# Adding the residual x to the partial output projection with accumulating DMAs instead of to the finished tiles on VectorE

## The chip, the cores and the metric

The kernel runs on one core of a Trainium2 chip. The metric is the device time of one execution in microseconds (us); a kernel's time is the median of its runs. An engine is named as in the profile: PE is TensorE (PEld its weight loads), DVE is VectorE, ACT is ScalarE, POOL is GpSimd, SP is SyncE. SPq is the queue of DMAs that SP issues.

## The reference

Two sequences, `x_sample` (1024 tokens) and `x_prompt` (512 tokens), each of width 2048, go through one layer and a final norm with the same weights:

```python
def mixer_layer(x, norm_g, w_in, w_dw, b_dw, ln_g, ln_b, w_pw, sink, w_out):
    h = rms_norm(x, norm_g)
    z = h @ w_in                       # split: conv value, glu, gate; q, k, v, attention gate
...
    conv_out = conformer_conv(c_val, c_glu, ...) * silu(c_gate)
    attn_out = banded_sink_attention(q, k, v, sink) * silu(a_gate)
    mix = concatenate([conv_out, attn_out], axis=-1) @ w_out
    return x + mix

def encoder(x, ...):
...
    return rms_norm(x, final_norm_g)
```

All is float32. The change touches one term only: the `x +` in the last line of `mixer_layer`, for `x_sample`.

## The kernel before, in words

Everything is held transposed: a tile has 128 channels on its partitions and tokens along its free dimension. Every float32 operand of a matmul is split into a high and a low part (`Encoder.parts`, lines 434 to 442: ACT copies x into the high part, L438, and DVE subtracts, L439), and a product is three matmuls, high by high, high by low, low by high.

The first sequence (`sample`, `x_sample`) has its large products in `Unit`s (class at line 91). A unit takes two blocks of 128 output channels, two halves of 512 tokens and eight blocks of the 2048 input channels, and computes this two by two by two product with seven products instead of eight (a Strassen-like scheme: sums of weights are made on DVE, L138, and sums of the tokens' operands are made ahead and kept in DRAM). Each of the seven products is twelve matmuls on one PSUM bank (`product`, matmul at L191; banks a, b and c, of which a product of the same unit uses one again). Behind the first matmuls of the next product, `tap` copies the bank to SBUF on ACT (L217) or adds it to a tile there on DVE (`add`, L237). A product that goes on in the same bank has to wait for that copy. Four tiles of 128 by 512 come out of a unit.

Since a unit covers only eight of the sixteen blocks of input channels, there are two units per pair of output blocks. The first one's four tiles are partial sums and are stored to DRAM (`finish`, line 240: `e.store(part, d)`, L432). The second one is `total`: `finish` issues an accumulating DMA on POOL's queue that adds the stored partial tile to the tile in SBUF (`add_into`, L429), and puts the rest of the work into the list `later` with a count. `turn_over` (line 468) is called once per product, lowers the counts, and takes the next step of an entry whose count is up.

The output projection of the first sequence (class `Mix`, line 1119) is eight pairs of output blocks, and so two runs of eight units: `over[0]` with `last` false, on the attention half of the input channels, then `over[1]` with `last` true, on the convolution half. While the first run is on PE, attention of the second sequence runs between its matmuls, and `conv_sums` (line 1165; `block_sums` L1138 to L1141) makes the sums of the convolution half. In the second run the count is `LANDING + 1` = 5 products. When it is up, `project` (L1213) does what is left: it has issued the load of the x tile on SP (L1217) when the accumulating DMA was issued; now DVE adds x (L1220), SP stores the finished tile to `y_d`, and in the next steps ACT squares it (L1227, or L1231 for the first tile) and DVE adds the squares to a running sum (L1229) for the final norm. `Mix.finish` later scales the stored tiles.

Buffers: the tiles that come out of PSUM are taken in turn from two rings of four buffers, `g` and `u` (`Encoder.E`, line 405). `u` also holds attention's queries (loaded at L1005) and outputs (copied at L1066), `g` a difference of weights (L138) in the first run, and both the sums of `block_sums`. The ring `p` of four holds the x tiles, attention's probabilities and operands on their way in. A buffer is used again when all that reads it is done, the store's DMA too.

The order of the instructions on each engine is fixed when the program is built, from the order and the priorities in which they are written: `urgently` and `high_priority` move taps and weight preparation forward, and lanes (`Lane`) hand out side work by an estimated cost per matmul. On SP's queue the DMAs are issued in that fixed order; one that waits for its data holds those behind it.

Of the kernel before, what the change touches and what calls it, by code (L numbers as in the profile page):

```python
# [10 lines left out]
ALU = mybir.AluOpType  # L11
# [22 lines left out]
W = 512  # L34
# [10 lines left out]
NF, NA, NG, NU, NP = 7, 4, 4, 4, 4  # L45
# [45 lines left out]
class Unit:  # L91
# [148 lines left out]
    def finish(self, n):  # L240
        e = self.e
        part, d = self.part[n[0]][n[1]], self.d.pop(n)
        if self.total:

            e.add_into(d, part)
            e.later.append([self.landing, self.done(n[0], n[1], d)])
        else:
            e.store(part, d)


class Plain(Unit):
# [402 lines left out]
class Sequence:  # L654
# [416 lines left out]
    def units(self):  # L1071

        e, w = self.e, self.e.a["w_in"]
        e.low = {}

        def both(cols, name, done):
            part = [[e.tc.dram_tile([P, W], F32, name=f"part_{name}_{t}{c}") for c in range(2)] for t in range(2)]
            keep = [e.tc.dram_tile([P, ND, P], F32, name=f"low_{name}_{c}") for c in range(2)]
            for c in range(2):
                e.low[cols[c]] = (keep[c], c)  # L1080
            return lambda g, last, kind=Unit: kind(e, w, cols, 2 * HALF * g, part, done if last else None, keep if g else None)

        def each(first, second):
            return lambda t, c, z: (first, second)[c](t, z)

        conv = [both((GLU + i, VAL + i), f"conv{i}", self.gated(i)) for i in range(NC)]
        gates = []
        for i in range(0, NC, 2):
            done = each(self.silu_of(self.gate_d[i]), self.silu_of(self.gate_d[i + 1]))
            gates.append(both((GATE + i, GATE + i + 1), f"gate{i}", done))  # L1090
        rest = gates[:2] + [
            both((K + g, V + g), f"kv{g}", each(self.rotate(self.k_d[g]), self.value_of(g))) for g in range(2)
        ]
        for h in range(HEADS):
            turn = self.rotate(self.q_d[h // GROUP][:, h % GROUP])
            rest.append(both((Q + h, AG + h), f"q{h}", each(turn, self.silu_of(self.ag_d[h]))))
        return conv, rest + gates[2:]
# [21 lines left out]
class Mix:  # L1119
# [77 lines left out]
    def units(self):  # L1197
        e = self.e
        out = []
        for o in range(0, ND, 2):  # L1200
            part = [[e.tc.dram_tile([P, W], F32, name=f"part_out{o}_{t}{c}") for c in range(2)] for t in range(2)]
            done = lambda t, c, z, o=o: self.project(o + c, t, z)

            def one(g, last, o=o, part=part, done=done):
                u = Unit(e, e.a["w_out"], (o, o + 1), 2 * HALF * g, part, done if last else None)
                u.late = True
                u.landing = LANDING + 1
                return u

            out.append(one)  # L1210
        return out

    def project(self, o, t, z):  # L1213
        e, nc = self.e, self.e.nc
        cols = slice(t * W, t * W + W)
        x = e.PT("p", NP, [W])
        nc.sync.dma_start(x, self.seq.xT[o][:, cols])  # L1217

        def steps():
            nc.vector.tensor_tensor(z, z, x, ALU.add)  # L1220
            e.store(self.y_d[o][:, cols], z)
            yield
            if not self.summed:
                self.sv = e.F([2, W])
            s = self.sv[:, t]
            if t in self.summed:
                nc.scalar.activation(x, z, AF.Square)  # L1227
                yield
                nc.vector.tensor_tensor(s, s, x, ALU.add)  # L1229
            else:  # L1230
                nc.scalar.activation(s, z, AF.Square)  # L1231
            self.summed.add(t)
            yield

        return steps()
# [615 lines left out]
```

## Time and profile before

| what | value |
|---|---|
| median of 3 runs | 2130.25 us |
| lowest and highest | 2127.07 and 2131.83 us |
| the profiled execution's own time | 2123.9 us |
| its span, first to last instruction | 2122.1 us |
| mean granted TensorE clock | 0.998 |
| DMA | 465.17 MB, 219 GB/s over the span |
| SP's queue (hardware), POOL's queue (software) | 60.6% and 9.0% of 16 engines |

A line of a group of instructions reads: source line, engine, operation, tile written <- tiles read, shapes, count, then busy us and mean ns of one, then the idle time of the engine just before them and what released it. In a timeline the first two numbers are the start and the duration in us, and the brackets at the end hold the idle time before and its releaser. In the list of waits the numbers are the us in total, how often, and the longest. In a table by stages each engine has its busy us and its number of instructions; then come the granted clock, the mean busy share of the 16 DMA engines and GB/s. A row of DMA issues has the count, the size and the median us from issue to landing.

### The profile page before, as it was taken

To read this page: it belongs to the slowest core of one execution; us is meant where nothing else is said; L and a number is where in the kernel's file an instruction comes from. 1 tells how busy PE (TensorE), PEld (TensorE's weight loads), DVE (VectorE), ACT (ScalarE), POOL (GpSimd) and SP (SyncE) were. 2 spreads that over 40 slices of the span, in tenths; PEclk is the share of its full clock that TensorE was granted. 3 is DMA by queue.
4 is the path that set the end of the run, shared out by engine and by line. 5 is a ranking of instruction groups with operands and counts; after the bars stand their busy time and mean duration, and the time that the engine had idled before them with its cause. 6 is when DMAs were issued, how large, how long until landed. Compare 5 with 4: busy or idle time off the path is not lost. (4 is left out here: it accounts for less than half of the span.)

```text
span 2122.1 us, 26838 instructions
## 1 busy us (share of the span) xinstructions
PE 2080.0 (98%) x9330; PEld 1709.6 (81%) x9330; DVE 1710.3 (81%) x2611; ACT 1064.6 (50%) x1736; POOL 105.1 (5%) x124
## 2 busy tenths in 40 slices
PE   8999999999999999899999999999999989999998
PEld 7878888888888888688888888878888867888886
DVE  8758799988899999899987776677899667987543
ACT  7475445333554444544556766345544564563232
POOL 0001110000011111000000000000000001110000
PEclk9999999999999999999999999999999999999999
DMA  8888878754677767754464547987765369799952
GB/s 286 310 286 243 231 179 277 265 190 155 227 215 178 185 161 194 240 183 144 151 219 157 192 157 235 323 291 255 249 238 199 105 208 269 192 306 314 309 172 80
DMA packets 236408, 465.17 MB, mean 219 GB/s; under 512 B 22128, under 2 KB 79856, under 8 KB 236272
## 3 DMA queue, kind: packets, MB, share of 16 engines
q1 hardware_dynamic: 218992, 431.99, 60.6%
q0 software_dynamic: 17280, 31.46, 9.0%
q8 instruction: 73, 1.20, 0.2%
q14 instruction: 63, 0.52, 0.1%
HBM read 319.19 MB, written 144.18 MB: 218 GB/s over the span
## 5 line engine op out<-in xcount | busy, mean ns | idle before, releaser
L191 PE MATMUL a<-t,hl 128*128 128x512 f32 x2640 | 634.3, 391 | 15.5 <-ACT u L217 6.0
L191 PEld LDWEIGHTS a<-t,hl 128*128 128x128 f32 x2640 | 494.7, 188 | 123.4 <-ACT u L217 9.2
L438 ACT ACTIVATE hl<-raw 128x1024 fp32r<-128x1024 f32 (+1 forms) x330 | 296.2, 898 | 367.8 <-DVE raw L138 66.7
L439 DVE TENSOR_TENSOR hl<-raw,hl 128x1024 fp32r<-128x1024 f32 (+1 forms) x330 | 337.6, 1023 | 171.0 <-ACT hl L438 167.0
L906 DVE SCALAR_TENSOR_TENSOR f<-f,c_w_dw,f 128x1024 f32<-128x1024 f32 (+1 forms) x464 | 456.0, 1011 | 1.8 <-ACT f L901 1.6
L578 PE MATMUL a<-t,hl 128*128 128x512 f32 x1344 | 329.0, 394 | 2.6 <-DVE f L848 2.2
L191 PE MATMUL c<-t,hl 128*128 128x512 f32 x1320 | 320.1, 390 | 1.6 <-ACT g L217 0.9
L578 PEld LDWEIGHTS a<-t,hl 128*128 128x128 f32 x1344 | 248.8, 188 | 53.8 <-DVE f L848 2.6
L191 PEld LDWEIGHTS c<-t,hl 128*128 128x128 f32 x1320 | 247.4, 188 | 54.0 <-ACT g L217 1.8
L578 PE MATMUL c<-t,hl 128*128 128x512 f32 x672 | 167.4, 395 | 0.0
L578 PE MATMUL b<-t,hl 128*128 128x512 f32 x672 | 162.2, 392 | 0.8 <-DVE hl L439 0.8
L191 PE MATMUL b<-t,hl 128*128 128x512 f32 x660 | 161.1, 390 | 0.0
L578 PEld LDWEIGHTS b<-t,hl 128*128 128x128 f32 x672 | 125.1, 188 | 26.1 <-DVE hl L439 1.2
L578 PEld LDWEIGHTS c<-t,hl 128*128 128x128 f32 x672 | 124.2, 188 | 24.5
L191 PEld LDWEIGHTS b<-t,hl 128*128 128x128 f32 x660 | 123.4, 188 | 25.1
L217 ACT ACTIVATE u<-a 128x512 f32<-128x512 f32 x114 | 67.3, 592 | 77.7 <-PE a L191 64.5
L217 ACT ACTIVATE g<-a 128x512 f32<-128x512 f32 x106 | 62.9, 593 | 80.8 <-PE a L191 68.9
L1534 PE MATMUL a<-hl,t 128*128 128x512 f32 x192 | 74.3, 390 | 0.0
L438 ACT ACTIVATE a<-pt 128x512 fp32r<-128x512 f32 x64 | 38.0, 594 | 62.5 <-PE pt L1058 62.3
L1038 ACT ACTIVATE p<-p,tiny 128x384 f32<-128x384 f32 (+1 forms) x96 | 54.5, 569 | 28.3 <-DVE tiny L1035 19.5
L346 ACT ACTIVATE hl<-raw 128x1024 fp32r<-128x1024 f32 x44 | 46.4, 1053 | 41.1 <-PE a L578 12.7
L439 DVE TENSOR_TENSOR a<-pt,a 128x512 fp32r<-128x512 f32 x64 | 43.9, 686 | 25.3 <-ACT a L438 24.9
(318 smaller groups left out, 2528.2 us busy)
## 6 DMA issues: line engine op xcount, KB each, us to landing
raw<-w_in SPq DMA_DIRECT2D x171, 512.0 KB, 5.0
raw<-w_out SPq DMA_DIRECT2D x64, 256.0 KB, 4.2
raw<-w_out SPq DMA_DIRECT2D x31, 512.0 KB, 4.7
raw<-w_pw SPq DMA_DIRECT2D x24, 512.0 KB, 4.8
p<-xT_s SPq DMA_DIRECT2D x40, 256.0 KB, 4.8
f<-x_s SPq DMA_DIRECT2D x16, 512.0 KB, 7.2
f<-y_d SPq DMA_DIRECT2D x16, 512.0 KB, 5.8
y_s<-f SPq DMA_DIRECT2D x16, 512.0 KB, 4.5
```

Source lines behind the costliest of these rows:

```text
L191: nc.tensor.matmul(acc, hl[:, l, o, j, :], toks[j][:, r], start=name in FRESH and j == 0 and q == 0, stop=name in LAST and j == HALF - 1 a ...
L217: nc.scalar.activation(t, bank, AF.Copy)
L346: e.nc.scalar.activation(t[:, 0], raw, AF.Copy)
L438: nc.scalar.activation(hi, x, AF.Copy)
L439: nc.vector.tensor_tensor(lo, x, hi.bitcast(F32), ALU.subtract)
L578: nc.tensor.matmul(job.acc[0], hl[:, l, kk // HALF, kk % HALF, :], r, start=i == 0 and p == 0, stop=i == nk - 1 and p == 2,)
L906: nc.vector.scalar_tensor_tensor(t, h[:, j : j + T], w(j), t, ALU.mult, ALU.add)
L1038: nc.scalar.activation(p[:, 0:n], p[:, 0:n], AF.Exp, bias=nm[:, h : h + 1], accum_out=l[:, h : h + 1])
L1534: nc.tensor.matmul(acc, self.mix[self.KS[i]][:, m, b * P : (b + 1) * P], part[l].rearrange("p a b -> p (a b)"), start=i == 0 and p == 0, s ...
```

## The change

In the first run of the output projection each finished partial tile gets an accumulating DMA on POOL's queue that adds the x tile from the input in DRAM to it. Its store is put into `later` with the count of five products, as an entry of its own with one step (`put`). In the second run `project` no longer loads x and no longer adds it: the finished tile is stored as it is, and the tile of the `p` ring is only taken where a square is written into it.

```diff
@@ -244,8 +244,18 @@
 
             e.add_into(d, part)
             e.later.append([self.landing, self.done(n[0], n[1], d)])
+        elif self.base:
+
+            e.add_into(d, self.base(*n))
+            e.later.append([self.landing, self.put(part, d)])
         else:
             e.store(part, d)
+
+    base = None
+
+    def put(self, part, d):
+        self.e.store(part, d)
+        yield
 
 
 class Plain(Unit):
@@ -1205,6 +1215,8 @@
                 u = Unit(e, e.a["w_out"], (o, o + 1), 2 * HALF * g, part, done if last else None)
                 u.late = True
                 u.landing = LANDING + 1
+                if not last:
+                    u.base = lambda t, c: self.seq.xT[o + c][:, t * W : t * W + W]
                 return u
 
             out.append(one)
@@ -1213,17 +1225,15 @@
     def project(self, o, t, z):
         e, nc = self.e, self.e.nc
         cols = slice(t * W, t * W + W)
-        x = e.PT("p", NP, [W])
-        nc.sync.dma_start(x, self.seq.xT[o][:, cols])
 
         def steps():
-            nc.vector.tensor_tensor(z, z, x, ALU.add)
             e.store(self.y_d[o][:, cols], z)
             yield
             if not self.summed:
                 self.sv = e.F([2, W])
             s = self.sv[:, t]
             if t in self.summed:
+                x = e.PT("p", NP, [W])
                 nc.scalar.activation(x, z, AF.Square)
                 yield
                 nc.vector.tensor_tensor(s, s, x, ALU.add)
```

## The prediction

> **What bounds the kernel now.** I read the head of the page, then the busy time of the engines by stage, then what TensorE waited for, then the instructions in order of time around those waits. The profiled execution took 2123.9 us (its span is 2122.1), 6.35 us under the median of 2130.25. The sum is made against that execution, and its difference in us is put onto the median.
>
> ```profile
> span 2122.1 us, 26838 instructions
> PE 2080.0 (98%) x9330; PEld 1709.6 (81%) x9330; DVE 1710.3 (81%) x2611; ACT 1064.6 (50%) x1736; POOL 105.1 (5%) x124
> ```
>
> PE is busy for all but 42 us. Work on DVE, SP or the DMA engines counts only where it makes PE wait. The first sequence's output projection is two runs of eight units: the first from about 1553 to 1735 us (it writes the partial tiles), the second to 1890 us (it completes them). By stage (the first is where sums of the convolution half are also made, the third is the switch between the runs, the fourth the second run):
>
> ```profile
> core 0: us, PE busy (x) PEld busy (x) DVE busy (x) ACT busy (x) POOL busy (x), PEclk, DMA share, GB/s
> 1553.00:1620.00 67.00, 65.55 (x299) 53.20 (x298) 63.94 (x110) 31.30 (x57) 0.00 (x0) 1.00 0.76 262
> 1620.00:1710.00 90.00, 90.00 (x419) 74.52 (x418) 60.18 (x112) 42.83 (x82) 0.00 (x0) 1.00 0.33 110
> 1710.00:1750.00 40.00, 34.47 (x143) 26.45 (x142) 28.46 (x44) 27.74 (x51) 0.86 (x1) 0.96 0.74 249
> 1750.00:1900.00 150.00, 146.85 (x648) 120.24 (x647) 126.93 (x194) 86.46 (x139) 27.01 (x31) 1.00 0.89 247
> ```
>
> The second run leaves PE idle for 150 - 146.85 = 3.15 us, the switch for 5.5, the first run for about 1.5 before 1620 and for nothing after. What PE waited for from 1560 to 1920 us:
>
> ```profile
> PE a L191 <- ACT hl L438: 2.8, 1, 2.8
> PE a L191 <- ACT g L217: 2.3, 1, 2.3
> PE a L191 <- ACT u L217: 2.1, 1, 2.1
> PE c L191 <- ACT g L217: 0.9, 2, 0.7
> ...
> 1720.79 8.52 PE L191 MATMUL a<-t,hl 128*128 128x512 f32 x36 [2.08 <-ACT u L217]
> 1743.01 0.73 PE L191 MATMUL a<-t,hl 128*128 128x512 f32 x2 [2.82 <-ACT hl L438]
> ```
>
> The 2.1 and the 2.8 lie in the switch, the 2.3 and the 0.7 in the second run.
>
> **What is taken out of the second run.** 32 additions on DVE and 32 loads of x:
>
> ```profile
> L1220 DVE TENSOR_TENSOR u<-u,p 128x512 f32<-128x512 f32 x16 | 10.8, 687 | 9.3 <-DMA p<-xT_s 8.3 <-DMA u<-part_out 1.0
> L1220 DVE TENSOR_TENSOR g<-g,p 128x512 f32<-128x512 f32 x16 | 10.8, 685 | 0.4 <-DMA p<-xT_s 0.4
> q1 hardware_dynamic: 13276, 28.37, 58.2%
> q0 software_dynamic: 4320, 7.87, 31.5%
> u<-part_out POOLq DMA_DIRECT2D x16, 256.0 KB, 6.7
> part_out<-u SPq DMA_DIRECT2D x16, 256.0 KB, 2.7
> ```
>
> The additions are 21.6 us of DVE, and 8.7 us in which DVE stood waiting for x. The queue rows are of 1755 to 1900 us, 145 us long. A plain transfer costs the sixteen engines 0.582 x 145 / 28.37 = 2.97 us per MB, 0.78 us for a tile of 0.262 MB. An accumulating one costs 0.315 x 145 / 7.87 = 5.80 us per MB, 1.52 us for a tile. So 32 x 0.78 = 25 us of DMA time leave the second run, and 32 x 1.52 = 49 us come into the first.
>
> What that is worth on PE is read from its one long wait there:
>
> ```profile
> 1782.46 0.69 DVE L1220 TENSOR_TENSOR u<-u,p 128x512 f32<-128x512 f32 x1 [3.45 <-DMA p<-xT_s]
> 1794.30 0.69 DVE L138 TENSOR_TENSOR raw<-raw 128x512 f32<-128x512 f32 x1
> 1795.02 1.06 ACT L438 ACTIVATE hl<-raw 128x1024 fp32r<-128x1024 f32 x1 [2.49 <-DVE raw L138]
> 1796.50 0.58 ACT L217 ACTIVATE g<-a 128x512 f32<-128x512 f32 x1
> 1797.13 3.04 PE L191 MATMUL a<-t,hl 128*128 128x512 f32 x12 [2.34 <-ACT g L217]
> ```
>
> DVE stands 3.45 us for a late x, then has no pause but 0.4 us (x again) until the weight difference at 1794.30, ACT waits 2.49 us for that, and the copy out of PSUM that PE needs is queued on ACT behind it. Without the addition the 3.45 us and the additions' own 0.69 us each are gone from that chain, more than the 2.34 us at its end: I take 2.3 us as gained. What is late next there are the loads of the convolution rows, which the next DVE step needs; they lose the competition of the x loads. Of the other 0.8 us in the second run I take half, since the 0.7 comes from ACT's copy order and not from x: gain 2.3 + 0.4 = 2.7 us, at least 0 (if the convolution rows hold DVE as long), at most 3.15 (all idle time of the stage). The Square keeps its tile of the p ring and is only allocated later: nothing.
>
> **What is added to the first run.** POOL issues 32 more transfers of 0.87 us, 28 us, on an engine that has no instruction in the first two stages: nothing. DMA: four accumulates per unit of 21 us are 6.1 us, a share of 0.29. From 1620 to 1710 that makes 0.62, covered; before 1620 it makes 1.05, so there loads come later. The weights are loaded two or more steps ahead, and the sums being made are wanted at 1716 us only: I take nothing, and 3 us as the upper bound.
>
> The store now waits five steps. The second run shows how long that is:
>
> ```profile
> 1759.00 0.88 POOL L429 DMA_DIRECT2D u<-part_out  x1 [7.34 <-DVE u L237]
> 1771.76 0.32 SPq L432 DMA_DIRECT2D y_d<-u  x1
> ```
>
> 12.8 us between an accumulate's issue and the store. The accumulate lands in 6.7 us, so the store does not wait on SP, and the weight loads queued behind it on SP are not held. But each of the 32 partial tiles keeps its buffer (g or u, four of each) 12.8 us longer than now. These buffers are already short in the first run, since there u also holds attention's queries and outputs, and both rings hold the sums that are made before 1620:
>
> ```profile
> 1577.08 0.58 SPq L1005 DMA_DIRECT2D u<-q_d  x1
> 1577.75 0.58 SPq L432 DMA_DIRECT2D part_out<-u  x1
> 1586.14 0.92 SPq L432 DMA_DIRECT2D msum_S<-u  x2
> 1588.32 0.60 ACT L217 ACTIVATE u<-a 128x512 f32<-128x512 f32 x1 [6.35 <-DMA msum_S<-u]
> 1589.97 2.89 PE L191 MATMUL a<-t,hl 128*128 128x512 f32 x12
> ...
> 1601.13 0.60 ACT L217 ACTIVATE u<-c 128x512 f32<-128x512 f32 x1 [0.32 <-PE c L191]
> 1626.30 0.60 ACT L217 ACTIVATE u<-a 128x512 f32<-128x512 f32 x1 [0.95 <-PE a L191]
> ```
>
> At 1588.32 the copy of a finished product waited until a sum's store had left its u buffer. The four u were a query tile, one partial tile, and the two sums stored from 1586.14. The tile stored at 1577.75 was free by then; after the change it is kept to 1577.75 + 12.8 + 2.7 = 1593.3. With it five tiles want four buffers, the copy can start when the query tile is let go at about 1591, ends 0.6 us later, and the product at 1589.97, which writes the bank that the copy reads, starts 1.6 us late; if it must wait for the partial tile itself, 3.9 us. I take 2 us per event. Counting tiles along the trace in this way I find two more places, the P5 copy near 1601 us (sums again) and the copy at 1626 us (a query tile and an output at once); at one of three other products can go first. So 2 x 2 = 4 us, bounds 0 (PE always has another product to go on with) and 10 (five events, the other sums and the end of attention too).
>
> **The switch.** The last four partial tiles of the first run are finished while the second run's operands are loaded, and PE's 2.8 us ends on those loads:
>
> ```profile
> 1725.84 0.32 SPq L432 DMA_DIRECT2D part_out<-u  x1
> 1730.02 0.32 SPq L432 DMA_DIRECT2D part_out<-g  x1
> 1736.00:1740.00 4.00, 4.00 (x19) 3.14 (x17) 3.78 (x6) 3.09 (x6) 0.86 (x1) 1.00 1.00 369
> 1740.00:1744.00 4.00, 0.92 (x3) 0.30 (x2) 3.97 (x7) 3.21 (x6) 0.00 (x0) 1.00 1.02 281
> 1744.00:1748.00 4.00, 3.85 (x10) 3.06 (x11) 2.63 (x6) 1.29 (x3) 0.00 (x0) 0.57 0.91 331
> 1746.06 0.69 DVE L138 TENSOR_TENSOR raw<-a,raw 128x512 f32<-128x512 f32 x1 [1.36 <-DMA a<-w_out]
> ```
>
> Four accumulates are 4 x 1.52 = 6.1 us of the DMA engines, four stores only move within the stage. The stage has a share of 0.74, 10 us free, but is full from 1736 on. Bounds: 0, if the free time takes them, and 6.1, if all of it is put before the last weight load. I take 2 us: the two tiles of 1725.84 and 1730.02 are accumulated close enough to the full stretch (3.0 us), and part of that load's lateness is its buffer, not the DMA.
> The Trainium skill ("DMA: Bandwidth & Descriptors", section "Anatomy of one DMA — SWDGE (gpsimd) path") gives a transfer from POOL a moving part of bytes over 436 GB/s, 0.6 us for such a tile; by that the four would be an estimated 2.4 us and the switch's price under 1, and the sum 1 us lower. The queue row above says 1.52 us for an accumulate, and I go by it.
>
> **Sum.** -2.7 + 4 + 2 = +3.3 us: 2127.2 for the profiled execution, 2133.5 on the median. A measurement of this kernel tells about 0.2%, 4.3 us, from no change, so this is within it.
>
> **The rivals.**
> Slower: the g and u buffers bind. For it: the copy at 1588.32 that waits for a buffer today, and that nothing shortens the hold of 12.8 us. Against it: PE has products of two other banks, and g has no query tiles. It decides from the third event on: five events of 2 us, 10, with the switch at 3 and a gain of 2.7, give +10.3, 2140.6.
> A stall longer than these also lowers the clock: behind the 2.8 us at 1743 the granted clock was 0.57 for 4 us, 1.7 us lost, and behind the 2.3 us at 1797 it was not lowered. "TensorE: Matmul & The Clock Gate" of the Trainium skill (section "Part 1: The HAM clock gate") puts the drop at an idle window of about 3.4 us; the trace has it earlier.
> Faster: the order of the copies changes with the new waits, no event reaches PE, the second run loses all of its 3.15 us, and the 2.1 us at 1721, where a copy stood behind attention's, goes too: -5.2, 2125.0. For it: DVE is busy for 126.93 of 150 us there, and 21.6 of it goes. Against it: nothing in the change touches the 2.1.
> No effect: x is still late work for some other wait in the second run, and the first run hides everything: 2130.
>
> **Chances.** The forecast 0.40, slower 0.37, faster 0.20, no effect 0.03. The forecast's own range is 2130 to 2134.5. The range that leaves out 2 in 10 goes from 2125 (nearly all of the faster case) to 2141 (the slower case at its price). Faster by over 0.2% 0.20, within 0.2% 0.43, slower 0.37.
>
> **What would show it.** Right: no row of p from x in the second run, the 3.45 us of DVE and the 2.34 us of PE gone; POOL issues from 1553 us on; the software queue's share of the first run up by 49 us; waits of the L217 copies on stores of part_out, and PE waits of 1 to 2 us behind them before 1630 us; the switch about 2 us longer. Wrong: the first run as short as now (the buffers have room), or the second run still idle for 3 us (something else was as late), or new waits of SP behind an accumulate.

## The result and the profile after

The changed kernel takes 2143.12 us (median of 4 runs, 2140.49 to 2146.97), the kernel before beside it 2131.04 (4 runs, 2127.07 to 2132.33). The ratio is 1.0057, 95% interval [1.0042, 1.0072]: 12.1 us slower, 9.6 us above the predicted 2133.5 and 2.1 us above the range. The profiled execution took 2141.12 us (span 2139.4) against 2123.9: 17.2 us more. The profile of before is of an execution some 7 us under the median of its kernel, that of after 2.0 us under its own, so that the stage sums below come out about 5 us above the difference of the medians. Two executions at a much lower granted clock, one of e12 (2602.03 us, clock 0.752) and one of the kernel before beside e5 to e8 (2984.17 us), are left out of the ratios.

The table by stage of the kernel after, with the same windows as before:

```profile
1553.00:1620.00 67.00, 57.88 (x245) 46.12 (x244) 54.78 (x94) 26.66 (x50) 8.75 (x10) 0.95 0.88 264
1620.00:1710.00 90.00, 90.00 (x414) 75.14 (x413) 64.36 (x112) 42.92 (x79) 14.78 (x17) 1.00 0.69 171
...
1750.00:1900.00 150.00, 140.89 (x607) 113.68 (x606) 114.53 (x174) 89.70 (x146) 25.28 (x29) 0.97 0.78 200
```

Before 1620 PE is busy for 57.88 us where it was busy for 65.55, and its granted clock is 0.95 where it was 1.00; the DMA share went from 0.76 to 0.88. From 1620 to 1710 PE is full, as before, though the DMA share has doubled from 0.33 to 0.69. So the loss of the first run lies wholly ahead of 1620. What PE waited for from 1540 to 1930:

```profile
PE a L191 <- ACT hl L448: 9.3, 3, 5.5
PE c L191 <- ACT u L217: 4.6, 1, 4.6
PE a L191 <- ACT u L217: 4.0, 2, 2.0
PE c L191 <- ACT t L448: 3.0, 2, 2.0
```

The four longest rows of before (the prediction shows them) were 2.8 us for hl, 2.3 and 0.9 for copies into g and 2.1 for a copy into u. The waits for copies into g were, but for 0.2 us, those of the second run. They are gone: PE doesn't wait at all in the second run now. The three largest rows of what ACT waited for from 1553 to 1625 are waits for DMAs:

```profile
ACT u L217 <- DMA part_out<-u: 7.2, 1, 7.2
ACT u L217 <- DMA msum_S<-u: 6.2, 1, 6.2
ACT g L217 <- DMA part_out<-g: 5.8, 1, 5.8
```

Two copies out of PSUM now wait for a buffer until the store of an earlier partial tile has left it. In order of time, with what DVE and PE did beside them:

```profile
1575.91 0.69 DVE L138 TENSOR_TENSOR g<-raw,raw 128x512 f32<-128x512 f32 x1 [2.10 <-DMA part_out<-g]
...
1577.14 0.60 ACT L217 ACTIVATE g<-a 128x512 f32<-128x512 f32 x1 [5.79 <-DMA part_out<-g]
1578.31 1.22 PE L191 MATMUL a<-t,hl 128*128 128x512 f32 x2 [2.64 <-ACT hl L448]
...
1593.47 0.60 ACT L217 ACTIVATE u<-a 128x512 f32<-128x512 f32 x1 [6.23 <-DMA msum_S<-u]
...
1602.79 0.86 POOL L439 DMA_DIRECT2D u<-xT_s  x1 [2.74 <-DVE tiny L1037]
...
1607.53 0.72 PE L191 MATMUL a<-t,hl 128*128 128x512 f32 x2 [1.20 <-ACT hl L448]
...
1610.17 0.32 SPq L442 DMA_DIRECT2D part_out<-u  x1
...
1615.14 0.60 ACT L217 ACTIVATE u<-c 128x512 f32<-128x512 f32 x1 [7.18 <-DMA part_out<-u]
...
1615.79 4.38 PE L191 MATMUL c<-t,hl 128*128 128x512 f32 x11 [4.55 <-ACT u L217]
```

At 1578.31 PE waits for operands (hl) that ACT made only after the copy that stood for g; the weight difference that they are made of (the g at 1575.91) had itself waited 2.10 us for the store of a g tile. At 1615.79 PE waits 4.55 us for the copy itself, because the product wants the bank that it reads. The copy at 1593.47 is the one that the prediction worked out (1588.32 before): it waits 6.23 us for a sum's store as it did before (6.35), and no PE wait follows it. Ahead of the 1.20 us at 1607.53 ACT was at work for attention and waited for no buffer.

What the stores waited for on SP's queue, over the whole execution:

```profile
SPq L442 <- DMA g<-xT_s: 62.8, 16, 8.7
SPq L442 <- DMA u<-xT_s: 57.4, 16, 7.3
```

All 32 stores came to the head of SP's queue before their accumulate had landed, and stood there for 120 us together. In the timeline above one accumulate into u is issued at 1602.79, and the store of a u tile leaves at 1610.17, 7.4 us later, not 12.8.

Where the time lies can be followed along the copies at L217, of which every trace has 295, in the same order but for a few neighbours that change places. This is the start of a copy minus the start of the same copy before, as the change over a stretch: to the copy at 1549.4 us of before (ahead of all that the change touches), from there to the one at 1691.2 (first run), to the one at 1778.5 (switch), to the one at 1885.4 (second run), and to the end. The rows of the experiments stand in the same table.

```
us              to 1549  first run  switch  second run  rest   sum
after              +0.9      +11.3    +9.5        -3.7  -0.9  +17.2
e1_hold_only       +6.2      +17.5    +3.7        -3.6  +0.4  +24.1
e2_pool_store      -1.7      +20.4    +8.6        -3.7  -1.1  +22.5
e3_dram_accumulate +1.8       +6.1    +4.2        -3.7  -0.9   +7.5
e4_no_x            +0.9       -0.2    +0.5        -3.7  -0.9   -3.4
e5_quiet           +2.0       +0.0    -0.5        -3.6  +0.6   -1.6
e6_u5              +1.3       +9.3    +8.2        -3.6  -0.8  +14.5
e7_before_u5       +6.6       -0.9    -0.6        +3.5  +0.4   +9.0
e8_tail            +3.9       -0.3    +9.9        +1.0  -0.2  +14.3
e9_five_of_each    +4.1       +7.7   +11.9        -3.6  -1.0  +19.1
e10_before_five    +7.2       -1.2    +4.3        -0.4  +5.3  +15.2
e11_plain_loads    +6.3       +1.1    +0.7        -3.7  -0.0   +4.4
e12_head           +0.6      +13.0    -0.6        -3.6  -0.1   +9.3
```

The first column shows how far single executions differ ahead of all that was changed, up to 6.3 us over 1549 us (e7, e9 and e10 have other buffers there too). The column of the second run is the steadiest: -3.6 or -3.7 wherever no x is loaded early in the second run.

### The profile page after: what moved, and what is told of

The parts are those of the page before. It is cut to its first block, busy times and chain, and to the rows that moved or that the text cites. A ratio compares the mean times of both kernels' runs of the same rounds, so it can differ in the third digit from the quotient of the medians.

```text
span 2139.4 us, 26823 instructions
## 1 busy us (share of the span) xinstructions
PE 2086.0 (98%) x9330; PEld 1714.1 (80%) x9330; DVE 1692.7 (79%) x2579; ACT 1064.3 (50%) x1736; POOL 133.0 (6%) x156
## 4 chain that ended last, share of the span: by engine, by line
PE 74%; issue 12%; DMA 6%; DVE 4%; POOL 2%; ACT 1%; SPq 0%; POOLq 0%; ACTq 0%; DVEq 0%
PE a L191 17%; PE a L588 13%; PE c L191 9%; PE c L588 7%; PE b L588 7%; PE b L191 4%; PE a L1544 2%; PE s L1544 2%; PE pv L1063 2%; PE s L1034 2%; PE s L191 2%; PE pt L1068 1%; POOL u L439 1%; PE b L1544 1%; PE c L1544 1%
## 5 line engine op out<-in xcount | busy, mean ns | idle before, releaser
L191 PE MATMUL a<-t,hl 128*128 128x512 f32 x2640 | 636.9, 392 | 20.4 <-ACT hl L448 9.3
L217 ACT ACTIVATE u<-a 128x512 f32<-128x512 f32 x114 | 67.5, 593 | 82.9 <-PE a L191 65.4
L217 ACT ACTIVATE g<-a 128x512 f32<-128x512 f32 x106 | 62.9, 593 | 82.4 <-PE a L191 69.1
```

Of the source, the lines that this page charges most:

```text
L191: nc.tensor.matmul(acc, hl[:, l, o, j, :], toks[j][:, r], start=name in FRESH and j == 0 and q == 0, stop=name in LAST and j == HALF - 1 a ...
L217: nc.scalar.activation(t, bank, AF.Copy)
```

## The experiments

Three theories went into them. B: a partial tile keeps its g or u buffer until its accumulate and its store are done, and copies out of PSUM wait for the buffer. S: SP's queue is held by stores that wait for accumulates, and the loads behind them are late. D: the accumulates load the DMA engines, so that everything else lands later.

**Stores at once, buffers still held (e1).** The x is added to the tile after its store, so that nobody reads it; x is left out of the result.

```diff
-            e.add_into(d, self.base(*n))
-            e.later.append([self.landing, self.put(part, d)])
+            e.store(part, d)
+            e.add_into(d, self.base(*n))
```

> Leaves x of the first sequence out of the output: each partial tile is stored on SP at once, as in the kernel before, and x is then accumulated into the tile in SBUF, where nobody reads it. So the buffers are held for a store and an accumulate (about 2.7 + 6.7 us), and SP's queue waits for no accumulate. Theory B (the g and u buffers held by the accumulates cost the first run 12 us): the first run loses 8 to 12 us, the switch 0 to 2, the second run gains 3.7, in all 5 to 10 us slower than before. Theory S (the stores that wait on SP for the accumulate hold the loads and stores queued behind them): nothing is lost in the first run and at the switch, in all 2 to 4 us faster than before. Theory D (the 49 us of DMA time of the accumulates delay the loads): as slow as the changed kernel, 10 to 13 us.

Measured: 2145.11 us, ratio 1.0072 [1.0049, 1.0094]. No store waits for an accumulate on SP any more, and yet the first run loses 17.5 us, more than any theory gave. The waits for DMAs of ACT at L217 from 1553 to 1632, the first two, now name the accumulate itself:

```profile
ACT u L217 <- DMA u<-xT_s: 10.6, 1, 10.6
ACT g L217 <- DMA g<-xT_s: 6.6, 1, 6.6
```

So S is not needed for the loss of the first run; buffers held by accumulates are enough, with the load that the accumulates bring (no run holds a buffer without that load). One thing took the place of SP's queue: here the accumulates stand on POOL until their stores have landed (two of them for 15.8 us from 1553 to 1632), which holds the buffers longer still. At the switch the loss falls from 9.5 to 3.7 us: there S has a share. What is gone of PE's waits from 1712 to 1800 is most of the 3.0 us for t and one of two 2.0 us waits for a copy into u; the wait for hl stays (5.7 us here, 5.5 in the change, 2.8 before).

**The stores on POOL's queue (e2).**

```diff
-        self.e.store(part, d)
+        self.e.nc.gpsimd.dma_start(part, d)
```

> The changed kernel with the stores of the partial tiles issued on POOL's queue behind the accumulates, so that SP never waits for an accumulate. Theory B: the buffers are held as long, the first run still loses 10 to 12 us; the switch at most 2; the second run gains 3.7; in all 7 to 10 us slower than before. Theory S: the first run and the switch lose at most 2 us, in all 2 to 4 us faster than before. Theory D: 10 to 13 us slower.

Measured: 2150.53 us, ratio 1.0099 [1.0075, 1.0123], the slowest of all and beyond what any theory gave. PE's longest wait from 1553 to 1632:

```profile
PE c L191 <- ACT u L217: 10.5, 1, 10.5
```

SP is free, but POOL's queue now has the stores that wait (54.7 and 54.2 us for accumulates into g and u from 1553 to 1800), and an accumulate behind such a store starts late: the hold grows, and the first run loses 20.4 us. In the switch PE waits 4.0 us for a copy into g, so the 8.6 us there are not a test of S.

**No buffer held, no wait on SP (e3).** The tile is stored at once, and x is accumulated onto the stored tile in DRAM, at the same places on POOL.

```diff
-            e.add_into(d, self.base(*n))
-            e.later.append([self.landing, self.put(part, d)])
+            e.store(part, d)
+            e.add_into(part, self.base(*n))
```

> Each partial tile is stored on SP at once, as before, and x is accumulated by POOL onto the stored tile in DRAM. No buffer is held and SP waits for no accumulate; the DMA work stays. Theories B and S: the first run as before, the switch 0 to 2 us longer, the second run gains 3.7, in all 1.5 to 4 us faster than before. Theory D: the first run and the switch still lose 5 us or more, in all slower than before.

Measured: 2136.28 us, ratio 1.003 [1.0016, 1.0043]. About half of the first run's loss is left (6.1 of 11.3) and 4.2 at the switch. Neither B in its narrow form nor S can do this; the stores themselves have become slower. The stores of e3 from 1553 to 1632, the last number being us from issue to landing:

```profile
msum_S<-u SPq DMA_DIRECT2D x8, 256.0 KB, 5.6
msum_S<-g SPq DMA_DIRECT2D x8, 256.0 KB, 5.6
part_out<-g SPq DMA_DIRECT2D x7, 256.0 KB, 3.9
part_out<-u SPq DMA_DIRECT2D x6, 256.0 KB, 5.1
```

and the same of before:

```profile
part_out<-u SPq DMA_DIRECT2D x8, 256.0 KB, 3.2
msum_S<-u SPq DMA_DIRECT2D x8, 256.0 KB, 3.8
msum_S<-g SPq DMA_DIRECT2D x8, 256.0 KB, 2.5
part_out<-g SPq DMA_DIRECT2D x7, 256.0 KB, 3.3
```

By these medians a store frees its buffer 0.6 to 3.1 us later than it did. D acts through the buffers too, and along the copies most of the 6.1 us come at one place:

```profile
1606.38 0.60 ACT L217 ACTIVATE u<-c 128x512 f32<-128x512 f32 x1 [3.22 <-DMA part_out<-u]
...
1607.03 1.65 PE L191 MATMUL c<-t,hl 128*128 128x512 f32 x3 [3.62 <-ACT u L217]
```

This is the same copy as the one at 1615.14 of the changed kernel; the store that it waited for was issued at 1599.49 and took 6.8 us to land. In the changed kernel itself the medians of these four rows are 2.4 to 3.8 us, as before (2.5 to 3.8), though the store behind the copy at 1615.14 took 4.9; e3's 6.1 us can't be taken over as the load's part of its 11.3.

**The gain alone (e4).** x is left out altogether (no accumulate in the first run, no load in the second).

> Leaves x of the first sequence out altogether: neither loads and additions in the second run nor accumulates in the first. It prices what the removal alone is worth. All theories: the first run and the switch as before, the second run without idle time, 3 to 4.5 us faster than before.

Measured: 2122.87 us, ratio 0.9971 [0.9958, 0.9983]. First run and switch are as before, the second run gains 3.7 us, and PE has no wait in it. This is about the most that moving x could bring.

**Later, when the engines are free (e5).** Tiles of the units 0 to 11 (a unit is numbered by its first output block: 0, 2, to 14) are stored at once. Their x is accumulated onto the stored tiles, but only during units 6 to 13: a small copy on POOL reads a finished tile there, and two accumulates follow it. Units 12 and 14 load x late as before.

```diff
         else:
+            self.release(d)
             e.store(part, d)
+            e.held.append((part, self.base(*n)))
...
+    def release(self, d):
+        e = self.e
+        if self.quiet and e.held:
+            e.nc.gpsimd.tensor_copy(e.small(1), d[:, 0:1])
+            c = list(e.nc.cur_bb.bb.instructions)[-1]
+            with e.tc.issue_after(c):
+                for _ in range(min(2, len(e.held))):
+                    e.add_into(*e.held.popleft())
```

> Twenty-two of the 24 stores of units 0 to 11 (two per pair of tiles) are as in the kernel before, issued at once; x is added to the stored tiles in DRAM by transfers that start only in units 6 to 13, after the first run's loads of weights have come down; units 12 and later load x late as before. Buffers (B) and load (D): the first run is as before (0 to +1 us), the switch too (0 to +1), and the second run keeps most of its gain (-2 to -3.7): -1 to -4 us, ratio 0.998 to 0.9995. If it is instead the mere 2 MB and more of accumulating transfers that cost, wherever they lie (a second rival, in which any stretch of this stage stalls under them), the quiet stretch loses 3 us or more and the sum is no faster than before.

Measured: 2122.53 us (9 runs), ratio 0.9974 [0.996, 0.9987]: faster than the kernel before, and by the times level with the kernel that has no x at all. Its stages:

```profile
1553.00:1620.00 67.00, 65.46 (x296) 53.15 (x296) 63.93 (x110) 31.42 (x57) 0.65 (x2) 1.00 0.77 261
1620.00:1710.00 90.00, 90.00 (x421) 74.55 (x419) 61.30 (x111) 42.37 (x78) 28.94 (x36) 1.00 0.80 183
```

The 24 accumulates raise the DMA share of the quiet stretch to 0.80 (0.33 before), and PE stays full there. The transfers cost nothing in that place, so the rival that accumulates stall PE wherever they lie falls. (In the changed kernel too PE is full there, with 17 accumulates into SBUF.)

**A fifth u buffer (e6, e7).** Room for it comes from the attention mask, which holds other numbers in both kernels.

```diff
-NF, NA, NG, NU, NP = 7, 4, 4, 4, 4
+NF, NA, NG, NU, NP = 7, 4, 4, 5, 4
```

> The changed kernel with five u buffers in place of four, with the room for it taken from the attention mask (which holds other numbers, so that the mask is left out of what is computed). B: the stalls of the first run that end on a u buffer (4.6 and 2.0 of the 8.4 us of waits, and the lower clock that follows) go or shrink, the first run loses 3 to 7 us in place of 12. S and D: the first run still loses 10 to 13 us, because neither SP's queue nor the transfers' load has changed. To be read against e7_before_u5, not against the kernel before.

> The control for e6: the kernel before with five u buffers and the mask left out in the same way. All theories: within 3 us of the kernel before, since no stall of the output projection in it ends on a u buffer; what the fifth buffer gives in earlier stages shows here and is subtracted.

Measured: e6 2141.73 us, ratio 1.0058 [1.0039, 1.0077]; e7 2129.14, ratio 0.9998 [0.9984, 1.0012]. The first run still loses 9.3 us in the trace (10.2 against the control's -0.9), where B gave 3 to 7: that expectation failed. The waits of ACT show why:

```profile
ACT g L217 <- DMA part_out<-g: 11.7, 3, 5.7
ACT u L217 <- DMA part_out<-u: 5.7, 1, 5.7
```

The waits have gone over to g, which is as short. (Of the waits that B was to take away, the 2.0 us ones for a copy into u lie at the switch, at 1732.98 and 1739.59, and not in the first run.)

**Only the later units (e8).** Accumulates for units 6 to 14, the rest as before.

```diff
-                if not last:
+                if not last and 6 <= o < 16:
```

> Accumulates x only for units 6 and later of the first half, that is after the first run's stalls; units 0 to 5 are stored at once and load x late as in the kernel before. B and D: the first run is as before (0 to +1 us), the switch still loses (+4 by load alone, up to +9.6 if the stores that stand on SP before the next loads of weights do it), the second run gains little or nothing because the late x of units 0 to 2 are still there (0 to -1): +4 to +9 us. If the switch's 9.6 us are only what the first run's stalls pass on (a rival), the switch loses nothing: -1 to +1 us.

Measured: 2133.64 us, ratio 1.0019 [1.0006, 1.0031]. The first run is as before, and the switch loses 9.9 us in the trace all the same: what is lost at the switch isn't handed on from the first run. There PE waits, from 1725 to 1785:

```profile
PE a L191 <- ACT hl L448: 5.2, 1, 5.2
PE a L191 <- ACT u L217: 2.9, 1, 2.9
PE c L191 <- ACT t L448: 2.8, 3, 2.0
```

and SP in the same stretch:

```profile
SPq L442 <- DMA u<-xT_s: 6.8, 2, 6.0
SPq L442 <- DMA g<-xT_s: 6.4, 1, 6.4
```

The operands t are made from loads that stand on SP behind these stores:

```profile
1746.01 0.32 SPq L442 DMA_DIRECT2D part_out<-g  x1
1746.42 0.38 SPq L796 DMA_DIRECT2D p<-msum_S  x1
...
1749.30 0.63 ACT L448 ACTIVATE t<-p 128x512 fp32r<-128x512 f32 x1 [2.82 <-DMA p<-msum_S]
```

The wait for hl is also there where no store waits for an accumulate on SP (5.7 us in e1, 6.0 in e3), so that it doesn't need SP's queue. By its times the kernel loses 4.0 us (0.19% of 2130.72), and its profiled execution was 4.6 us above its median, so that the switch's size is known only as 4 to 10 us.

**Five buffers of each (e9, e10).** Five u, five g, one a fewer, and no mask.

```diff
-NF, NA, NG, NU, NP = 7, 4, 4, 4, 4
+NF, NA, NG, NU, NP = 7, 3, 5, 5, 4
```

> The changed kernel with five u and five g buffers (one a buffer fewer, and the attention mask left out, to make room). With a fifth u alone the first run still lost about 11 us and its waits had gone over to the g buffers. B: with both, the waits of the activations of line 217 on transfers of g and u shrink to 5 us or less in the first run, and it loses 3 to 7 us, about what the accumulates on the stored tiles in DRAM left (6), all of it load. S, D or SP's queue as the cause in the first run: it still loses 10 to 13 us. The switch keeps its loss (4 to 10) in either case. To be read against e10_before_five.

> The control for e9: the kernel before with the same buffers and the mask left out. All theories: no stall of the output projection changes; the buffer a that is missing may cost up to 10 us in other stages, which is subtracted, stage by stage.

Measured: e9 2147.45 us, ratio 1.0094 [1.007, 1.0117]; e10 2140.2, ratio 1.0063 [1.0042, 1.0084]. Against its control the change costs 1.0094 / 1.0063, 0.31% in place of 0.57%; each ratio is uncertain by 0.2%, so the times alone don't decide. (The control itself lost more than the 10 us that were expected, 4.3 of them at the switch, where e9 loses 11.9.) In the trace the first run loses 7.7 us (8.9 against the control's -1.2), between what B gave (3 to 7) and the others (10 to 13). ACT's waits at L217 for stores of partial tiles, 5 us or less by B, were

```profile
ACT u L217 <- DMA part_out<-u: 7.8, 1, 7.8
ACT g L217 <- DMA part_out<-g: 4.7, 1, 4.7
```

A fifth buffer of each takes a part away and not all of the waits. Nor does it take away D or the stores' stand on SP (23.7 and 16.4 us from 1553 to 1632), both of which lengthen the hold. The number of buffers alone is not the whole cause.

**The same bytes as plain loads (e11).** Stores at once; POOL's queue loads the x tiles at the same places of the program into p, where nobody reads them (x is left out).

```diff
-            e.add_into(d, self.base(*n))
-            e.later.append([self.landing, self.put(part, d)])
+            e.store(part, d)
+            e.nc.gpsimd.dma_start(e.PT("p", NP, [W]), self.base(*n))
```

> Partial tiles stored at once, as before; POOL's queue loads the same 32 tiles of x at the same places, but as plain transfers into a buffer p that nobody reads (x left out of what is computed). If the load's share of the first run's loss (about 6 us of 12, from e3) lies in the accumulating form, whose tile takes about twice the engines' time of a plain one, the first run loses 1 to 4 us here; if in the added bytes and packets, 5 to 7 us. At the switch the buffers p are also wanted for the loads of the next sequence, so that its loss here tells nothing apart.

Measured: 2126.74 us, ratio 0.9989 [0.9974, 1.0004]. The first run loses 1.1 us, against 6.1 in e3. The queues from 1553 to 1632 (packets, MB, share of the 16 engines) of e11 and, in the second fence, of e3:

```profile
q1 hardware_dynamic: 9594, 19.55, 71.3%
q0 software_dynamic: 817, 2.71, 9.7%
```

```profile
q1 hardware_dynamic: 9168, 18.68, 67.0%
q0 software_dynamic: 1590, 2.90, 24.6%
```

For 7% more bytes the accumulating transfers take 2.5 times the engines' time (24.6 against 9.7%). (e3's go to DRAM; those of the change, into SBUF, are priced below and cost about as much.) That prices the form, but it doesn't show that the form makes the loss, though the time came out where the expectation put it. The plain loads wait for no finished tile and for a free p buffer, and so did not run at the same times: eight were issued from 1565.79 to 1573.51, and the next only here:

```profile
1626.39 2.47 POOL L250 DMA_DIRECT2D p<-xT_s  x4 [52.34 <-PE pt L1068]
```

So no plain load was under way at the place where e3's copy waited (1606.38), and e11's 1.1 us arose right behind its first eight loads. Whether the same bytes in plain form would have cost less beside that copy was not tried.

**The units of e5, at the change's places (e12).**

```diff
-                if not last:
+                if not last and 0 <= o < 12:
```

> As the change, but only for units 0 to 11, the ones of e5, with their accumulates where the change has them; units 12 and later load x late as before. The first run loses its 11 to 13 us in full, the switch little (0 to +2, since no unit there accumulates), and the second run gains 3 to 3.7: +7 to +11 us, ratio 1.003 to 1.005. Against e5 it then shows that when the transfers run decides, not how many there are.

Measured: 2135.80 us (9 runs), ratio 1.0026 [1.0015, 1.0038], a little under what was expected. In the trace the first run loses 13.0, the switch nothing, the second run gains 3.6. The same 24 tiles cost 0.26% here and bring 0.26% in e5. The two differ in when the transfers run, in whether the store waits for them, and in whether they go to SBUF or to DRAM. e3 has no waiting store, goes to DRAM as e5 does and still loses, so the time at which they run has a share of its own.

The times agree with the trace's stages: e12 is +5.5 us (0.26% of 2129.2), and with the gain of e4 (6.2, 0.29% of 2130.29) the first run's price is 11.7. The whole change is +12.1, which leaves 6.6 for the switch. Each of the three figures is uncertain by 2.5 to 3 us, the remainder by some 5.

## Why the prediction was wrong

It put its 0.37 on the mechanism that came ("the g and u buffers bind", 2140.6) and 0.40 on a milder form of it. The measured time lies above both.

**The second run's gain** was right: the row of L1220 and its loads are gone, the two PE waits on the copy into g are gone, 2.7 us forecast and 3.7 measured (e4 alone: 3.7). The term was small by 1.0 us, and its upper bound of 3.15 was too low.

**"The store does not wait on SP, and the weight loads queued behind it on SP are not held"** failed. The 12.8 us were read from a store of the second run, which has DVE work ahead of it; in the first run all 32 came to SP's head before their accumulate had landed. The landing itself was read rightly (6.4 and 7.0 us in the median, 6.7 forecast), and the hold was no longer than forecast (from 1602.79 to the copy at 1615.14 it is 12.35 us, where I had 12.8 + 2.7). From the waiting stores came the part of the switch that I had not counted: 9.5 us where I took 2, and 3.7 in e1, where SP doesn't wait. The 2 us (bounds 0 to 6.1) were near the part that is left without waits on SP, 3.7 and 4.2 in e1 and e3. New waits of SP behind an accumulate were among the prediction's own signs of being wrong.

**"2 x 2 = 4 us" of buffer events** was the term most mis-sized: 11.3 in the trace, 11.7 by the times. The mechanism held; of my three places one came, and at three times its price. The event that I had worked out (1588.32) costs nothing, nor does the copy at 1626. The "P5 copy near 1601 us" is the one at 1615.14 after the change: it waited 7.18 us and PE 4.55, and the shift along the copies goes from 4.8 us ahead of it to 11.3 behind it, 6.5 where I took 2. Of those 4.8 us 4.3 come with a copy into g at 1577, which I had argued away ("g has no query tiles"). What mis-sized the term is the length of one wait: it is as long as the rest of an accumulate and a store, not the 1.6 to 2 us by which two holds overlapped in my count, and the lower clock comes on top.

**"I take nothing"** for the DMA engines ahead of 1620 failed. The share of 1.05 that the prediction had worked out was the warning. I asked which loads would be late; what came late in e3 was the stores that free buffers. There the accumulates cost 6.1 us in the first run with no buffer held longer by the kernel's order, over my upper bound of 3. How much of this is in the change itself no run separates.

**The clock** was named and not priced in the events. Behind the waits of 2.64 and 4.55 us it was lowered, behind the 1.20 us at 1607.53 it was not:

```profile
1577.00:1582.00 5.00, 3.69 (x9) 2.98 (x10) 4.51 (x8) 2.64 (x5) 1.76 (x2) 0.66 0.94 291
1607.00:1612.00 5.00, 3.71 (x15) 2.74 (x15) 5.00 (x10) 0.96 (x2) 0.00 (x0) 1.00 0.96 324
1615.00:1620.00 5.00, 4.21 (x11) 3.36 (x12) 2.65 (x4) 2.67 (x6) 0.89 (x1) 0.66 0.43 168
```

Before 1620 PE is idle for 7.7 us more (65.55 - 57.88), and a clock of 0.95 over 57.88 us takes 2.9 more: 10.6 of the 11.3. The Trainium skill ("TensorE: Matmul & The Clock Gate", section "Part 1: The HAM clock gate") puts the drop at an idle window of about 3.4 us; here it came behind 2.64 us, the granted clock being 0.66 over those 5 us, as behind the 2.8 us that the prediction showed.

**POOL's 28 us of issuing** cost nothing, as forecast: PE is full from 1620 to 1710 with 17 of them beside it.

Open: how the 11.3 us split between the buffers' hold, SP's stand and the load. e3 shows that the load can cost 6.1 with no hold, e1 that hold and load are enough without SP, e9 that the number of buffers is only a part of it; but the parts act on the same copies, and they need not add up. A kernel with SP held and no buffer held, one with buffers held and no accumulates, and one with plain transfers at the times of the accumulates were not tried.

## What to carry to other kernels

A step taken off a chain paid here only where the transfer that replaces it ran while the DMA engines had room and no tile's store waited for it: the same 24 tiles cost 0.26% beside a stage that was already loaded and gained 0.26% a few units later, beside PE at full work. Before a transfer is put between a tile and its store, add its landing to the hold of the tile's buffer and look at who stands behind that store on its queue; a copy out of PSUM that waits for a buffer can become a wait of PE nearly as long as the rest of the transfer (4.55 of 7.18 us here), or none at all (behind the 6.23 us at 1593.47). Ask when a store comes to the head of its queue: the gap between an accumulate and a store that has other work ahead of it, as in the second run here, doesn't tell it for one that has none.

## What the runs showed of the hardware

An accumulating transfer takes about twice the engines' time of a plain one. In the changed kernel, from 1553 to 1632, the queues and the issues are:

```profile
q1 hardware_dynamic: 8549, 17.17, 63.0%
q0 software_dynamic: 1650, 3.02, 23.3%
...
g<-xT_s POOLq DMA_DIRECT2D x7, 256.0 KB, 6.4
u<-xT_s POOLq DMA_DIRECT2D x6, 256.0 KB, 7.0
```

0.233 x 79 / 3.02 = 6.1 us of the sixteen engines per MB, on DRAM (e3) 0.246 x 79 / 2.90 = 6.7, and plain from the same queue (e11) 0.097 x 79 / 2.71 = 2.8. The packets are smaller too: 3.02 MB in 1650, 1.83 KB each, against 2.71 MB in 817, 3.3 KB each. I had the price per tile from the second run, 1.52 us, and it is 1.60 here.

The Trainium skill ("DMA: Bandwidth & Descriptors", section "SWDGE vs HWDGE vs iDMA") ties an accumulate during a transfer to DMAs that GpSimd issues, and the trace agrees as far as it goes: all 32 are issued by POOL, 0.87 us each, and go by the software queue.
